# A gated layer's values projected with tokens on the partitions, and a weight split moved to GpSimd

## The chip, the cores and the metric

The kernel runs on one core of a Trainium2 chip. The metric is the device time of one execution in microseconds (us). Three runs of the kernel before took 2728.38, 2730.65 and 2730.97 us, so the median is 2730.65 us.

## The reference

Two layers over a sequence of 1024 tokens of width 1024. Layer 0 mixes with dilated attention, layer 1 with a gated recurrence (HGRN2), and each is followed by a squared-ReLU MLP; every sub-layer ends in a layer norm of a scaled residual plus its output. The change is in the gated recurrence of layer 1:

```python
def hgrn2_mixer(x, w_in, w_out, norm_g, lb):
    B, S, _ = x.shape
    H, K, V, C = HGRN_HEADS, HGRN_DK, HGRN_DV, HGRN_CHUNK    # 8, 128, 128, 64
    q_raw, f_raw, i_raw = jnp.split(x @ w_in, [H * K, 2 * H * K], axis=-1)
    z = f_raw.astype(F32)
    log_f = jnp.logaddexp(jnp.log(lb), jnp.log1p(-lb) + jax.nn.log_sigmoid(z))
    key = (1.0 - lb) * jax.nn.sigmoid(-z)
    q = jax.nn.silu(q_raw.astype(F32))
    v = i_raw.astype(F32)
    ...
    b = jnp.cumsum(log_f, axis=3)                  # within each chunk of 64 tokens
    q_dec = q * jnp.exp(b)
    k_dec = key * jnp.exp(-b)
    a = jnp.where(causal, einsum('bhcid,bhcjd->bhcij', q_dec, k_dec), 0.0)
    o_intra = einsum('bhcij,bhcje->bhcie', a, v)
    kv = einsum('bhcjd,bhcje->bhcde', key * jnp.exp(b_last - b), v)
    # states: S[c+1] = decay[c] * S[c] + kv[c]
    o_inter = einsum('bhcid,bhcde->bhcie', q_dec, states)
    o = o_intra + o_inter, then an RMS norm over each head's 128 columns, times norm_g
    return o @ w_out
```

## The kernel before

Every large product is taken in three matmuls on a high and a low part: a tensor is split by ScalarE (ACT), which rounds it to the high part, and VectorE (DVE), which subtracts that from the raw tensor to get the low part (`split`, L147 to L149). The three are high x high, low x high and high x low. TensorE (PE) works through the whole program in this way: attention, its output projection with the layer norm, the first MLP, the gated layer, its output projection with the layer norm, and the second MLP. SyncE (SP) issues nearly all transfers. A scheduler fixes the order of each engine's instructions when the program is built; the chip then runs each engine's list in order and waits on semaphores. Tiles in on-chip memory come from one pool of 49 slots of 128x1024.

In the gated layer (`hgrn`, L1734) the input x lies as features on the partitions and tokens along the row, in two halves of 512 tokens. For each of the 8 heads three 512 KB weight tiles are loaded (`w_load`, tile `wr`, split into `wh` and `wl`): forget gate z, query q and value v. `proj` (L176) makes each product in two slots of 24 matmuls of 128x512, one per half, so a head has six slots. ACT copies each out of PSUM (`ze`, `qe`, `vTh`). All three come out with features on the partitions. Behind the second z slot follows the gate chain on ACT and DVE (L1865 to L1888), behind the second q slot the query chain (L1889 to L1899, ending in `qe`).

The work per head that needs these results is made in pieces (`head_pieces`, L1743), which are run one slot each beside the next head's projections: `trans` turns `vTh` and the decayed key (tile `ze`) with 8 PE transposes each (PSUM tile `hpt`) and two ACT copies each (into `vn` and `k2n`); `amat` makes the masked scores (`as`, copied under a mask into `aT` by DVE); `kv` makes 15 outer products (`kvps`), which DVE adds up into 15 states (`stA`, `stB`, L1777 to L1781); `omats` makes the output from `aT`, `vn` and the states (`ho`), followed by the RMS norm on ACT and DVE (`sq`, `rms`, `on`); `otr` transposes that (`opt`) and ACT scales it into `oN`, which for the first five heads is stored to DRAM and loaded again later (`onr`).

The output projection (`Out`, `outproj_ln`) needs `oN` of all heads as the stationary operand, split into `hoh` and `hol`, and the output weights, split in halves of 512 columns into `woh` and `wol` from the raw tile `wor`. While the last head's pieces are still outstanding, `stage_a` multiplies by the first `NKA[1]` = 7 heads only, and `tick` (L1148) puts the outstanding pieces between its groups of three matmuls; `fin` (L1209) adds the remaining heads and makes the layer norm. `NKA` = (6, 7) holds the number for the attention and the gated layer.

## Time and profile before

| | |
|---|---|
| median of three runs | 2730.65 us |
| the profiled execution | 2730.97 us |
| its span, from its first to its last instruction | 2729.2 us |
| TensorE busy | 2699.1 us (99%) |
| VectorE, ScalarE, GpSimd busy | 2052.6 (75%), 1404.6 (51%), 189.7 us (7%) |
| granted TensorE clock, mean | 0.999 of full speed |

The 1.77 us between the execution's time and its span lie outside the instructions. In the rows below the gated layer's projections run from about 1666 to 2006 us and its output projection from there to about 2107 us, on the span's own clock. A row of a timeline has a start, a duration, the engine, the line and the tiles (output <- inputs). A duration of a matmul is longer than its step to the next one, since they overlap in the array: what a matmul costs is the difference of two starts. A wait is given in square brackets with its releaser.

### The profile page before, as it was taken

To read this page: it belongs to the slowest core of one execution; us is meant where nothing else is said; L and a number is where in the kernel's file an instruction comes from. 1 tells how busy PE (TensorE), PEld (TensorE's weight loads), DVE (VectorE), ACT (ScalarE), POOL (GpSimd) and SP (SyncE) were. 2 spreads that over 40 slices of the span, in tenths; PEclk is the share of its full clock that TensorE was granted. 3 is DMA by queue.
4 is the path that set the end of the run, shared out by engine and by line. 5 is a ranking of instruction groups with operands and counts; after the bars stand their busy time and mean duration, and the time that the engine had idled before them with its cause. 6 is when DMAs were issued, how large, how long until landed. Compare 5 with 4: busy or idle time off the path is not lost.

```text
span 2729.2 us, 41117 instructions
## 1 busy us (share of the span) xinstructions
PE 2699.1 (99%) x14600; PEld 2229.9 (82%) x14600; DVE 2052.6 (75%) x3948; ACT 1404.6 (51%) x3021; POOL 189.7 (7%) x366
## 2 busy tenths in 40 slices
PE   8999999999999999999999999999999999999998
PEld 6888888888888778888888888888888888888887
DVE  7778878778788778776687686666578786677687
ACT  5655555555555626444554344555553644454443
POOL 1021221212122100000000000000000000000000
PEclk9999999999999999999999999999999999999999
DMA  8887868777799524554685743010232464487654
GB/s 332 278 261 226 265 193 259 231 243 246 235 302 313 185 85 168 191 193 151 204 311 188 242 147 116 32 63 32 74 128 108 151 224 166 152 298 244 220 179 126
DMA packets 215790, 529.41 MB, mean 194 GB/s; under 512 B 28096, under 2 KB 41664, under 8 KB 215584
## 3 DMA queue, kind: packets, MB, share of 16 engines
q1 hardware_dynamic: 197632, 484.64, 52.5%
q0 software_dynamic: 17952, 42.14, 5.4%
q8 instruction: 115, 1.88, 0.3%
q14 instruction: 91, 0.75, 0.1%
HBM read 402.63 MB, written 98.44 MB: 184 GB/s over the span
## 4 chain that ended last, share of the span: by engine, by line
PE 91%; DVE 4%; issue 2%; DMA 1%; ACT 1%; POOL 0%; SPq 0%; DVEq 0%; POOLq 0%; ACTq 0%
PE pmm L792 8%; PE pmm L794 8%; PE pmm L793 8%; PE pup L1342 7%; PE pup L1344 7%; PE pup L1343 7%; PE pdy L1489 4%; PE pdy L1492 4%; PE pdy L1493 4%; PE pdx L1489 3%; PE pdx L1492 3%; PE pdx L1493 3%; PE pmm L182 3%; PE pmm L184 3%; PE pmm L183 3%
## 5 line engine op out<-in xcount | busy, mean ns | idle before, releaser
L792 PE MATMUL pmm<-xh,H 128*128 128x512 f32 x1008 | 401.9, 399 | 10.2 <-ACT H L496 6.5
L793 PE MATMUL pmm<-xl,H 128*128 128x512 f32 x1008 | 394.6, 391 | 4.0 <-DVE xl L149 4.0
L794 PE MATMUL pmm<-xh,H 128*128 128x512 f32 x1008 | 395.2, 392 | 1.3 <-DVE H L505 1.1
L792 PEld LDWEIGHTS pmm<-xh,H 128*128 128x128 f32 x1008 | 190.1, 189 | 59.5 <-issue 8.5
L794 PEld LDWEIGHTS pmm<-xh,H 128*128 128x128 f32 x1008 | 189.9, 188 | 43.7 <-DVE H L505 3.4
L793 PEld LDWEIGHTS pmm<-xl,H 128*128 128x128 f32 x1008 | 190.4, 189 | 42.7 <-DVE xl L149 4.6
L1489 PE MATMUL pdy<-dT,dS 128*128 128x512 f32 x512 | 199.2, 389 | 0.0
L1492 PE MATMUL pdy<-dT,dS 128*128 128x512 f32 x512 | 199.2, 389 | 0.0
L1493 PE MATMUL pdy<-dT,dS 128*128 128x512 f32 x512 | 199.2, 389 | 0.0
L182 PE MATMUL pmm<-f0nh,wh 128*128 128x512 f32 x384 | 152.3, 397 | 0.0
L148 ACT ACTIVATE dS<-dr 128x512 fp32r<-128x512 f32 x192 | 119.2, 621 | 60.0 <-PE pdy L1493 25.9
L183 PE MATMUL pmm<-f0nl,wh 128*128 128x512 f32 x384 | 149.8, 390 | 0.0
L184 PE MATMUL pmm<-f0nh,wl 128*128 128x512 f32 x384 | 149.8, 390 | 0.0
L607 ACT ACTIVATE p<-p,stats 128x256 f32<-128x256 f32 (+1 forms) x256 | 118.3, 464 | 55.0 <-DVE stats L604 54.4
L149 DVE TENSOR_TENSOR dS<-dr,dS 128x512 fp32r<-128x512 f32 x192 | 131.6, 685 | 16.9 <-ACT dS L148 16.3
L148 ACT ACTIVATE dT<-dr 128x512 fp32r<-128x512 f32 x128 | 79.3, 624 | 86.6 <-DVE dr L1462 51.7
L604 DVE CUSTOM_DVE_ANT_0 p<-s,mask 128x256 f32<-128x256 f32 (+1 forms) x256 | 82.4, 377 | 44.9 <-PE s L576 44.9
L1303 ACT ACTIVATE H<-wc 128x512 fp32r<-128x512 f32 x128 | 76.9, 625 | 72.3 <-DVE wc L1296 42.1
L1493 PEld LDWEIGHTS pdy<-dT,dS 128*128 128x128 f32 x512 | 96.1, 188 | 20.0
L1489 PEld LDWEIGHTS pdy<-dT,dS 128*128 128x128 f32 x512 | 96.1, 188 | 20.0
L1492 PEld LDWEIGHTS pdy<-dT,dS 128*128 128x128 f32 x512 | 96.1, 188 | 19.9
L867 POOL DMA_DIRECT2D rot<-e x176 | 86.3, 496 | 281.2 <-DVE e L827 50.8
(438 smaller groups left out, 6905.1 us busy)
## 6 DMA issues: line engine op xcount, KB each, us to landing
xh<-xtd SPq DMA_DIRECT2D x138, 512.0 KB, 6.3
xl<-xtd SPq DMA_DIRECT2D x138, 512.0 KB, 6.5
dr<-hd SPq DMA_DIRECT2D x192, 256.0 KB, 4.0
dr<-in_w_down_dram SPq DMA_DIRECT2D x160, 256.0 KB, 4.8
wa<-in_w_up_dram SPq DMA_DIRECT2D x48, 512.0 KB, 3.8
rot<-e POOLq DMA_DIRECT2D x176, 128.0 KB, 6.4
wb<-in_w_attn_dram SPq DMA_DIRECT2D x36, 512.0 KB, 6.3
wa<-in_w_attn_dram SPq DMA_DIRECT2D x33, 512.0 KB, 5.5
```

The lines of the kernel that those rows point to most:

```text
L148: act(hi, raw, AF.Copy)
L182: nc.tensor.matmul(o, wh[:, k], xs.h(k), start=k == 0, stop=False)
L183: nc.tensor.matmul(o, wh[:, k], xs.l(k), start=False, stop=False)
L184: nc.tensor.matmul(o, wl[:, k], xs.h(k), start=False, stop=k == NK - 1)
L792: nc.tensor.matmul(o, wh, hi[k // 2][:, c], start=begin and k == 0, stop=False, skip_group_check=True)
L793: nc.tensor.matmul(o, wh, lo[k // 2][:, c], start=False, stop=False, skip_group_check=True)
L794: nc.tensor.matmul(o, wl, hi[k // 2][:, c], start=False, stop=end and k == 3, skip_group_check=True)
L1342: nc.tensor.matmul(o, wh, xf.h(b, k), start=begin and k == 0, stop=False, skip_group_check=True)
L1343: nc.tensor.matmul(o, wh, xf.l(b, k), start=False, stop=False, skip_group_check=True)
L1489: nc.tensor.matmul(o[q], h, T_[:, L], start=begin, stop=False, skip_group_check=True)
L1492: nc.tensor.matmul(o[q], h, T_[:, R], start=False, stop=False, skip_group_check=True)
L1493: nc.tensor.matmul(o[q], l, T_[:, L], start=False, stop=end, skip_group_check=True)
```

## The change

The weight columns for the values are taken out of the per-head tiles. They are handed in as a second tensor `w_hgrn_i`, in two batches of four heads; each batch is four 512 KB tiles (`wir`, split into `wih` and `wil`) that hold two of the eight blocks of 128 input features by 512 value columns. A new function `values(batch, t)` takes 128 tokens of x as the stationary operand and 512 value columns of four heads as the moving one, so the values come out with tokens on the partitions; eight calls make a batch, each with 24 matmuls of 128x512 and one ACT copy into `vn`. The transposes of `vTh` and their copies go. The first batch runs in head 0's slots (four token blocks ahead of its z and q, four behind), the second at the head of head 4; other heads have four slots. The pieces of a head now take seven slots and run over into the head after the next; one list of six steps is left for the output projection.

`NKA[1]` becomes 5, and heads 5 and 6 are taken into `stage_a` as their output is there. The second halves of the output weights are loaded and split within the first `stage_a`, and the low half of each output weight in the gated layer is made by GpSimd (POOL) instead of DVE, 16 subtractions of 128x512 in all. In the first MLP the tile that is loaded ahead is the first of the values' tiles.

```diff
-NKA = (6, 7)
+NKA = (6, 5)
...
             nc.sync.dma_start(raw[:, c], self.w_dram[k][:, c])
-            split(raw[:, c], hi[:, c], lo[:, c])
+            act(hi[:, c], raw[:, c], AF.Copy)
+            (nc.gpsimd if self.mixer else nc.vector).tensor_sub(lo[:, c], raw[:, c], hi[:, c].bitcast(F32))
...
-        for k in range(nka):
-            pr.split_w(k, 1)
+        if not pr.mixer:
+            for k in range(nka):
+                pr.split_w(k, 1)
...
                     tick()
+                if len(tiles) > 1 and pr.mixer:
+                    pr.split_w(k, 1)
...
-            self.order = [(hd, t) for hd in range(8) for t in (1, 0, 2)]
+            self.order = [(hd, t) for hd in range(8) for t in (1, 0)]
+            self.wi = {}
...
+        def prefetch_i(self, batch, u):
+            if (batch, u) not in self.wi:
+                self.wi[batch, u] = w_load(w_hgrn_i[batch][:, u * 1024:(u + 1) * 1024], "wi")
...
                     nc.tensor.matmul(kb[c % 2][:, (t % 4) * P:(t % 4 + 1) * P], st["k2n"][r, t * P:(t + 1) * P],
-                                     st["vn"][r, t * P:(t + 1) * P], start=True, stop=True, skip_group_check=True)
+                                     val(hd, t)[r], start=True, stop=True, skip_group_check=True)
...
-                if hd < SPILL[1] and j == 1:
-                    nc.sync.dma_start(ond[1, hd], oNt)
+                if j == 1:
+                    if hd < SPILL[1]:
+                        nc.sync.dma_start(ond[1, hd], oNt)
+                    oN.append(ond[1, hd] if hd < SPILL[1] else oNt)
...
             return [
-                [lambda: trans(vT, "vn"), lambda: amat(0), lambda: amat(1), lambda: trans(kd2, "k2n")],
+                [],
+                [lambda: trans(kd2, "k2n")],
+                [lambda: amat(0), lambda: amat(1)],
                 [lambda: kv(0), lambda: kv(1)],
-                [],
                 [omats],
                 [],
                 [lambda: otr(0), lambda: otr(1)],
-            ]
+            ][hd == 7:]
...
+        def values(batch, t):
+            if (batch, t // 2) not in vals:
+                vals[batch, t // 2] = U("vn")
+            o = bank("mm", "pmm")
+            x_, c = xs[t // 4], slice((t % 4) * P, (t % 4) * P + P)
+            for k in range(NK):
+                wh, wl = (w[:, (k % 2) * 512:(k % 2) * 512 + 512] for w in gw.wi[batch, k // 2])
+                nc.tensor.matmul(o, x_.h(k, c), wh, start=k == 0, stop=False)
+                nc.tensor.matmul(o, x_.h(k, c), wl, start=False, stop=False)
+                nc.tensor.matmul(o, x_.l(k, c), wh, start=False, stop=k == NK - 1)
+            act(vals[batch, t // 2][:, (t % 2) * 512:(t % 2) * 512 + 512], o, AF.Copy)
...
-        prefetch(0)
-        n = 0
+        for u in range(4):
+            gw.prefetch_i(0, u)
...
-            slots = [(t, h) for t in (1, 0, 2) for h in range(2)]
+            slots = [(t, h) for t in (1, 0) for h in range(2)]
             if hd == 0:
-                slots = [(1, 1), (0, 1), (2, 1), (1, 0), (0, 0), (2, 0)]
...
+                slots = [(2, 4), (2, 5), (2, 6), (2, 7), (1, 1), (0, 1), (1, 0), (0, 0), (2, 0), (2, 1), (2, 2), (2, 3)]
+            elif hd == 4:
+                slots = [(2, t) for t in range(8)] + slots
...
+                    if hd == 3:
+                        gw.prefetch_i(1, 2 * (1 - t) + h)
...
-    xs, late = ffn(0, xf, late, x1d, ln_ffn_g[0], ln_ffn_b[0], False, lambda: gw.prefetch(0),
+    xs, late = ffn(0, xf, late, x1d, ln_ffn_g[0], ln_ffn_b[0], False, lambda: gw.prefetch_i(0, 0),
...
-        "w_hgrn": cols(i["hgrn_w_in"][0]),
+        "w_hgrn": cols(i["hgrn_w_in"][0][:, :2 * D]),
+        "w_hgrn_i": i["hgrn_w_in"][0][:, 2 * D:].reshape(NK, P, 2, 512).transpose(2, 1, 0, 3).reshape(2, P, NK * 512),
```

On SP, at the start of the gated layer, the kernel before has this, where `wr` is a weight tile and `x3d` the first MLP's stored output:

```order
610 L1525 DMA x3d<-z 128x1024
611 L153 DMA wr<-in_w_hgrn_dram 128x1024
612 L1740 DMA smask<-in_smask_dram 128x1024
613 L1525 DMA x3d<-z 128x1024
614 L153 DMA wr<-in_w_hgrn_dram 128x1024 x2
615 L1525 DMA x3d<-z 128x1024
616 L153 DMA wr<-in_w_hgrn_dram 128x1024 x5
```

The changed kernel has, at the same place:

```order
610 L1530 DMA x3d<-z 128x1024
611 L154 DMA wir<-in_w_hgrn_i_dram 128x1024
612 L1750 DMA smask<-in_smask_dram 128x1024
613 L1530 DMA x3d<-z 128x1024
614 L154 DMA wir<-in_w_hgrn_i_dram 128x1024 x2
615 L1530 DMA x3d<-z 128x1024
616 L154 DMA wir<-in_w_hgrn_i_dram 128x1024
617 L154 DMA wr<-in_w_hgrn_dram 128x1024 x7
```

The four value tiles stand where the first four weight tiles stood, the fourth behind a store of `x3d`, and the weight tiles follow behind them.

On PE, where the last head's projections end, the kernel before goes over from `wh` and `wl` to the output weights `woh` and `wol` like this; `opt` and `as` belong to heads 6 and 7, `hpt` to head 7:

```order
7608 L184 MATMUL pmm<-f0nh,wl 128x512
7609 L1820 MATMUL opt<-ident,on 128x128 x8
7610 L1760 MATMUL as<-qe,ls 128x128 x8
7611 L194 MATMUL pmm<-woh,hoh 128x512
7612 L195 MATMUL pmm<-wol,hoh 128x512
...
7617 L196 MATMUL pmm<-woh,hol 128x512 x2
7618 L1752 MATMUL hpt<-ident,vTh 128x128 x8
7619 L196 MATMUL pmm<-woh,hol 128x512
```

In the changed kernel head 6's outer products `kvps` and its output `ho` stand at this place, the latter in pieces between three to six matmuls of the output projection:

```order
7591 L185 MATMUL pmm<-f0nh,wl 128x512
7592 L1782 MATMUL kvps<-vn,k2n 128x128 x15
7593 L195 MATMUL pmm<-woh,hoh 128x512
7594 L196 MATMUL pmm<-wol,hoh 128x512
7595 L197 MATMUL pmm<-woh,hol 128x512
7596 L1800 MATMUL ho<-vn,aT 128x128 x4
7597 L1804 MATMUL ho<-stA,qe 64x128 x5
7598 L195 MATMUL pmm<-woh,hoh 128x512
7599 L196 MATMUL pmm<-wol,hoh 128x512
7600 L1804 MATMUL ho<-stA,qe 64x128
```

Head 6's outer products and output, which ran beside head 7's projections, now run behind them, with 3 matmuls of the output projection between the two.

On DVE, the states of head 6 (`stA`, `stB`) stand ahead of head 7's gate chain (lines from L1871 on) in the kernel before:

```order
2741 L1778 COPY stA<-kvps 128x128
2742 L1780 SCALAR_TENSOR_TENSOR stA<-stA,dec,kvps 128x128 x6
2743 L1780 SCALAR_TENSOR_TENSOR stB<-stA,dec,kvps 128x128
2744 L1780 SCALAR_TENSOR_TENSOR stB<-stB,dec,kvps 128x128 x7
2745 L1871 SCALAR_TENSOR_TENSOR ls<-ze,a_18701 128x1024
2746 L1872 SCALAR_TENSOR_TENSOR ze<-ze,a_18701 128x1024
2747 L1876 TENSOR_SCALAR ls<-ls,hc_C,hc_A 128x1024
```

In the changed kernel they stand behind it, and two splits of the head outputs (`hol`) stand between:

```order
2743 L1917 TENSOR_TENSOR ls<-ls,a_18609 128x1024
2744 L1918 SCALAR_TENSOR_TENSOR a_18609<-smask,ls 128x1024
2745 L150 TENSOR_TENSOR hol<-onr,hoh 128x512
2746 L1921 TENSOR_TENSOR ze<-ze,a_18609 128x1024
2747 L150 TENSOR_TENSOR hol<-onr,hoh 128x512
2748 L1924 TENSOR_TENSOR ze<-a_18609,ze 128x1024
2749 L1788 COPY stA<-kvps 128x128
2750 L1790 SCALAR_TENSOR_TENSOR stA<-stA,dec,kvps 128x128 x6
2751 L1790 SCALAR_TENSOR_TENSOR stB<-stA,dec,kvps 128x128
```

The states of head 6 have moved from ahead of head 7's gate chain to behind it.

## Rows read from the trace of the kernel before

**Rows 1.** The page: busy us, share of the span and instructions per engine.

```profile
PE 2699.1 (99%) x14600; PEld 2229.9 (82%) x14600; DVE 2052.6 (75%) x3948; ACT 1404.6 (51%) x3021; POOL 189.7 (7%) x366
```

**Rows 2.** TensorE's waits, 1660 to 2110: releaser, us in total, times, longest.

```profile
PE as L1760 <- DVE qe L1898: 0.9, 1, 0.9
PE pmm L196 <- DVE hol L149: 0.4, 1, 0.4
```

**Rows 3.** Busy us (instructions) of the engines by stretch, granted clock, DMA share, GB/s.

```profile
core 0: us, PE busy (x) PEld busy (x) DVE busy (x) ACT busy (x) POOL busy (x), PEclk, DMA share, GB/s
1500.00:1600.00 100.00, 100.00 (x443) 82.83 (x442) 78.52 (x137) 41.66 (x82) 0.00 (x0) 1.00 0.67 222
1793.00:1836.00 43.00, 43.00 (x261) 36.51 (x260) 26.01 (x44) 23.59 (x34) 0.00 (x0) 1.00 0.13 47
...
2060.00:2110.00 50.00, 50.00 (x236) 40.90 (x235) 45.99 (x94) 15.55 (x41) 0.00 (x0) 1.00 0.38 140
```

**Rows 4.** PE timeline, heads 0 and 1: start, us, engine, line, operation, tiles, count.

```profile
1705.95 1.03 PE L1752 MATMUL hpt<-ident,vTh 128*128 128x128 f32 x8
1706.74 0.48 PE L182 MATMUL pmm<-f0nh,wh 128*128 128x512 f32 x1
1707.07 0.40 PE L183 MATMUL pmm<-f0nl,wh 128*128 128x512 f32 x1
...
1750.38 1.03 PE L1752 MATMUL hpt<-ident,vTh 128*128 128x128 f32 x8
1751.25 0.94 PE L1760 MATMUL as<-qe,ls 128*128 128x128 f32 x7
```

**Rows 5.** PE timeline at 1710, head 0: the wait for its query.

```profile
1710.28 0.39 PE L182 MATMUL pmm<-f0nh,wh 128*128 128x512 f32 x1
1711.55 1.16 PE L1760 MATMUL as<-qe,ls 128*128 128x128 f32 x8 [0.88 <-DVE qe L1898]
```

**Rows 6.** PE timeline at 2007, the first output projection tiles.

```profile
2007.28 0.39 PE L195 MATMUL pmm<-wol,hoh 128*128 128x512 f32 x1
2008.03 0.73 PE L196 MATMUL pmm<-woh,hol 128*128 128x512 f32 x2 [0.36 <-DVE hol L149]
```

**Rows 7.** PE timeline in head 6: eight score products, fifteen state products, next projection.

```profile
1988.68 1.95 PE L1790 MATMUL ho<-vn,aT 128*128 128x128 f32 x16
1990.56 0.98 PE L1794 MATMUL ho<-stA,qe 128*64 128x128 f32 x13
...
1992.45 0.50 PE L182 MATMUL pmm<-f0nh,wh 128*128 128x512 f32 x1
```

**Rows 8.** DVE by line, 1793 to 1837: count, busy us, mean ns, idle.

```profile
L1878 DVE TENSOR_TENSOR_SCAN a<-smask,ls 128x1024 f32<-128x1024 f32 x1 | 2.3, 2291 | 0.0
```

**Rows 9.** ACT by line in the same stretch.

```profile
L1753 ACT ACTIVATE vn<-hpt 128x512 f32<-128x512 f32 x2 | 1.1, 597 | 0.0
```

**Rows 10.** DVE timeline in head 6: first states, then the gate chain.

```profile
1976.88 0.29 DVE L1778 COPY stA<-kvps 128x128 f32<-128x128 f32 x1 [6.71 <-PE kvps L1772]
1977.29 2.26 DVE L1780 SCALAR_TENSOR_TENSOR stA<-stA,dec,kvps 128x128 f32<-128x128 f32 x6
...
1982.60 1.22 DVE L1871 SCALAR_TENSOR_TENSOR ls<-ze,a 128x1024 f32<-128x1024 f32 x1
```

**Rows 11.** POOL by line, whole span, and DVE's instructions on tile wol.

```profile
L1737 POOL MEMSET aT<- 128x1024 f32 x1 | 1.0, 954 | 658.5 <-DVE dT L149 658.5
masks.py:199 POOL TENSOR_SCALAR_AFFINE_SELECT ident<-ident 128x128 f32<-128x128 f32 x1 | 0.3, 285 | 0.0
...
L149 DVE TENSOR_TENSOR wol<-wor,woh x32: 667/687/693, 898.4 to 2035.9; 128x512 fp32r<-128x512 f32 x32
```

**Rows 12.** 512 KB weight tiles: landing, and SP's issues at the stage's start.

```profile
DMA to landing us min/median/max: 3.3/5.3/6.3
...
1661.67 1.21 SPq L153 DMA_DIRECT2D wr<-in_w_hgrn_dram  x2
...
1673.34 2.90 SPq L153 DMA_DIRECT2D wr<-in_w_hgrn_dram  x4
```

More of the change, by code (lines that the diff above doesn't have):

```diff
@@ L81, in trunk_kernel @@
     w_hgrn: bass.AP,
+    w_hgrn_i: bass.AP,
     w_hgrn_out: bass.AP,
@@ L1789, in omats @@
                     cs = slice(t % 4 * P, (t % 4 + 1) * P)
-                    nc.tensor.matmul(os[t // 4][:, cs], aTs[t // 4][:, cs], st["vn"][:, t * P:(t + 1) * P],
+                    nc.tensor.matmul(os[t // 4][:, cs], aTs[t // 4][:, cs], val(hd, t),
                                      start=t % 4 == 0, stop=False, skip_group_check=True)
@@ L1834, in hgrn @@
         oN = []
         pend = []
-        prefetch(0)
-        n = 0
+        for u in range(4):
+            gw.prefetch_i(0, u)
         for hd in range(8):
             e = {}
-            slots = [(t, h) for t in (1, 0, 2) for h in range(2)]
+            slots = [(t, h) for t in (1, 0) for h in range(2)]
             if hd == 0:
-                slots = [(1, 1), (0, 1), (2, 1), (1, 0), (0, 0), (2, 0)]
-                for i in range(3):
-                    prefetch(i)
+                slots = [(2, 4), (2, 5), (2, 6), (2, 7), (1, 1), (0, 1), (1, 0), (0, 0), (2, 0), (2, 1), (2, 2), (2, 3)]
+            elif hd == 4:
+                slots = [(2, t) for t in range(8)] + slots
@@ L1845, in hgrn @@
             seen = set()
             cur = {}
-            for t, h in slots:
-                bi = hd * 3 + (1, 0, 2).index(t)
-                prefetch(bi)
-                prefetch(bi + 1)
-                if t not in e:
-                    e[t] = U(("qe", "ze", "vTh")[t])
-                if bi == len(order) - 1 and h == 1 and hd:
-                    pre(oN)
-                o = proj(loaded[bi], xs[h])
-                act(e[t][:, h * 512:(h + 1) * 512], o, AF.Copy)
+            for n, (t, h) in enumerate(slots):
+                if t == 2:
+                    values(hd // 4, h)
+                    if n == 1:
+                        prefetch(hd * 2)
+                    if n == 2:
+                        prefetch(hd * 2 + 1)
+                else:
+                    bi = hd * 2 + 1 - t
+                    prefetch(bi)
+                    if bi % 8 != 7:
+                        prefetch(bi + 1)
+                    if t not in e:
+                        e[t] = U(("qe", "ze")[t])
+                    if hd == 7 and n == 2:
+                        pre(oN)
+                    o = proj(loaded[bi], xs[h])
+                    act(e[t][:, h * 512:(h + 1) * 512], o, AF.Copy)
+                    if hd == 3:
+                        gw.prefetch_i(1, 2 * (1 - t) + h)
@@ L1899, in hgrn @@
                     cur["qd"] = q
-            for i in range(3):
-                del loaded[hd * 3 + i]
+            for i in range(2):
+                del loaded[hd * 2 + i]
+            if hd % 4 == 0:
+                for u in range(4):
+                    del gw.wi[hd // 4, u]
             oNt = U("oN")
-            oN.append(ond[1, hd] if hd < SPILL[1] else oNt)
-            new = head_pieces(hd, cur["kd"], cur["kd2"], cur["qd"], e[2], cur["dec"], oNt)
-            pend = [(pend[i] if i < len(pend) else []) + new[i] for i in range(len(new))]
+            new = head_pieces(hd, cur["kd"], cur["kd2"], cur["qd"], cur["dec"], oNt)
+            pend = [(pend[i] if i < len(pend) else []) + (new[i] if i < len(new) else [])
+                    for i in range(max(len(pend), len(new)))]
         return oN, pend
```

5 lines of the change are left out of this document (4 added, 1 removed).

## The prediction

> **What bounds the kernel now.** I read the page first, then TensorE's waits, then the timeline where the change acts. The reader is to see that TensorE is busy for 2699.1 of 2729.2 us [rows 1], that in steady work its matmuls of 128x512 follow each other at 100 / 443 = 0.226 us at a granted clock of 1.00 [rows 3], and that in the whole stretch from 1660 to 2110 us, which holds the gated layer and its output projection, it waits twice, for 0.9 and 0.4 us [rows 2]. So within the stage only three things change the time: instructions of TensorE that go, these two waits, and new waits. VectorE is busy 26.0 of 43 us beside one head's projections, and ScalarE 23.6 [rows 3]: their work there is covered, and what is taken off them is worth nothing by itself. Behind the projections that is otherwise: from 2060 to 2110 VectorE is busy 46.0 of 50 us [rows 3].
>
> **Transposes.** The 8 transposes of `vTh` take 1751.25 - 1750.38 = 0.87 us where other small products follow, and 1706.74 - 1705.95 = 0.79 us alone, behind which the next matmul takes 0.33 instead of 0.23 us, so 0.89 [rows 4]. There is one such block per head: 8 x 0.87 = 7.0 us gone. The 384 matmuls for the values stay 384 of the same shape: 16 value blocks of 24 against 8 heads x 2 x 24. The 16 ACT copies of 597 ns [rows 9] go too, 9.6 us of an engine that is not awaited: nothing. The weight splits keep their number. In the steady heads a slot holds a small block as before, four per head, so the borders stay.
>
> **The two old waits.** Head 0's scores wait for `qe`: 1711.55 - 1710.28 = 1.27 us to the next start, less 0.23 for the matmul and 0.1 for the border, 0.95 us [rows 5]. After, four value blocks (4 x 5.4 us of matmuls) stand between head 0's query and its scores, so that wait goes: -0.95. Behind it the next head's query is not late: a head still has 96 matmuls, 21.7 us, and small products; the chain of 1024-wide steps and the 2.29 us scan [rows 8] that ran beside 43 us of work must fit into about 31.5, of which VectorE's work fills an estimated 27 (the 26.0 us of rows 3 with the third weight's share added). I take no wait there and 3 us as the far end. The wait at 2007.28 for the low half of a head's output, 2008.03 - 2007.28 - 0.23 = 0.5 us [rows 6], stood behind a subtraction of a weight on VectorE; with that on GpSimd it goes: -0.5.
>
> **Start of the stage.** The first value block needs all four value tiles, where the first z slot needed one. Tile 4 is issued where 1673.34 stands now, behind a store of `x3d` [rows 12]. It lands 3.3 to 6.3 us later, so at 1676.6 to 1679.6, is then split (about 2 us), and is needed when 6 of 8 feature blocks of three token blocks, which the scheduler has interleaved, are through: about 54 matmuls and the layer-norm transposes, some 14 us behind 1666, near 1680. I take +0.5 us between 0 and +5.
>
> **Small blocks that split up.** At the end of the projections `ho`, `as` and `opt` stand in pieces between single matmuls. I count 12 blocks against 8. A border costs 0.1 on leaving [rows 4] and at most as much on entering: +0.8, between 0.4 and 1.2.
>
> **End of the projections.** Here lies the uncertain term. With T the end of the last projection, head 6's `kvps`, `ho` and head 7's pieces now all stand behind it, where only head 7's stood. On TensorE 15 outer products (taken like the 15 state products, 1992.45 - 1990.56 = 1.9 us [rows 7]), 3 matmuls (0.7) and 4 score products (half of 1990.56 - 1988.68, 0.9 [rows 7]) put the first five state products at T + 3.5, done at T + 4.2. On VectorE the states now stand behind head 7's gate chain. That chain starts when z is out of PSUM, 14 us before T (two slots of 5.4, the blocks 0.9 and 2.8), runs through six ACT steps of about 1.1 us with the two `k2n` copies and two weight copies between, so that the scan starts near T - 2.4 and ends near T - 0.1; then two `hol` at 0.69 and two 1024-wide steps at 1.22 [rows 10, 11] end near T + 3.7. The copy (0.29) and four more states at 2.26 / 6 = 0.38 [rows 10] come at T + 5.6. What waits is 5.6 - 4.2 = 1.4 us, and up to 2.5 if an ACT step comes later; I take 2.0. Queued behind these state products are head 7's transposes and the whole output projection. Next, head 7's query: its chain ends near T + 15.3 on VectorE, behind head 6's norm, and its scores are due near T + 14.7: 0.65 (0 to 1.5). Then one weight's high half, late on ACT behind the query chain, 0.3, and head 7's `kvps`, which need a PSUM bank that ACT has to empty, one copy of 0.6 us: 0.65.
>
> **The lower halves on GpSimd.** The trace of before has no subtraction on GpSimd. The nearest rows are half of a 128x1024 memset, 0.48 us, and four times the 128x128 select, 1.14 us; VectorE takes 0.687 us for the same subtraction [rows 11]. A second input could double the select's: 2.3 us. Between 0.48 and 2.3 I take 1.2, near the select, which like it reads its data. Of the 16, those for the third head's first half and the fifth head's second half are needed within about 1 us of ACT's high half: 1.7 us of waiting at 1.2 (0 at 0.48, 4.6 at 2.3). The others have several matmul groups in front. By the Trainium skill, GPSIMD Engine Reference, section 3.1 (Elementwise — side-by-side cycle accounting), an add of two fp32 tensors took 1.96 times VectorE's time, since the two inputs share a read port; by that a subtraction here would be an estimated 1.35 us, and the two waits 2.0 instead of 1.7. No run here shows it yet.
>
> **Sum.** -7.0 - 0.95 - 0.5 + 0.5 + 0.8 + (2.0 + 0.65 + 0.3 + 0.65 + 1.7 = 5.3) = -1.85 us against the profiled execution's 2730.97 (span 2729.2 and 1.77 outside): 2729.1. The median of before is 2730.65, 0.3 lower than that execution, so I say 2729.0 us. About 0.2%, 5.5 us, is what a measurement of this kernel can tell from no change; this lies within.
>
> **Rivals.** *The cover holds.* The scheduler has ordered the pieces so that each state, query and low half is there in time, and the end of the projections costs 1 us instead of 5.3. For it: TensorE waited only 0.4 us there before [rows 2], and VectorE is rid of 16 x 0.687 = 11 us. Against it: the states stand behind the gate chain. The time would be 2729.0 - 4.3 = 2724.7, and 2722.5 with no wait and no new border: faster. *GpSimd and VectorE hold each other up* (slower). Each subtraction on GpSimd lengthens whatever two-input work VectorE has beside it. Of the 16, about 10 fall into the 25 us behind T, where VectorE is already what TensorE waits for; if each holds VectorE for its own 1.2 us, 12 us come on top of 5.3, some of it taken up by VectorE's lost 11 us of subtractions only later: 2729.0 + 8 to 12 = 2737 to 2741. From 7 us of such holding on, the change is slower. For it: VectorE's list there is one chain; against it: no row shows the two engines at work together. The Trainium skill, GPSIMD Engine Reference, section 1 (Specifications), says that GpSimd shares its SBUF interfaces with VectorE and that they contend with instructions of two SBUF inputs, which speaks for this rival; no row here bears it out or against it. *The start is late.* Tile 4 lands at the slow end and each tile's split queues behind the layer norm on VectorE: +5 instead of +0.5, 2733.5, still no change. *The values gain nothing*, because with x stationary the matmuls have another pitch: 384 x 0.01 us would be 4; both forms load 128x128 weights and move 512 columns, so I give it next to nothing.
>
> **How the numbers follow.** Forecast with its own spread (2725.2 to 2736.1): 0.52. The cover holds, or nearly: 0.25. GpSimd holds VectorE up: 0.15. Late start: 0.08, which counts as no change. So faster 0.25, same 0.60, slower 0.15. The range is 2722.5 (no new wait at all) to 2737.5 (just into the slower rival, and what all the upper ends of the known terms but the start's come to: -8.45 + 0.5 + 1.2 + 2.5 + 1.5 + 0.6 + 1.3 + 4.6 = 3.75 above the forecast's start from 2730.97, so 2734.7, with half of the late start).
>
> **What would show it.** In the trace after, the `hpt` blocks from `vTh` are gone and with them the wait for `qe` near 1711. TensorE's waits between the last projection and the layer norm name VectorE's `stA`, `qe` or the `wol` on GpSimd, in sum about 5 us; under 2 the first rival is right. The mean of the 16 `wol` on GpSimd is near 1.2 us, and VectorE's rows of 1024 beside them keep 1.22 us; if they grow, the second rival is right. A wait on `wih` or `wil` within the first 20 us of the stage shows the third. I am wrong in the main point if the states are in time, or if the steady heads wait at all.

## The result, and the profile after

The changed kernel takes 2740.59 us (median of 7 runs, 2738.18 to 2741.56) against 2730.65 us of the kernel before (7 runs, 2727.06 to 2735.45): a ratio of 1.0034, with a 95% interval of 1.0025 to 1.0044. The forecast was 2729.0 us within 2722.5 to 2737.5, no change. It is slower by 9.9 us.

The time ahead of the gated layer varies by some 10 us between executions in which that part is the same (the layer's first projection starts between 1661.4 and 1670.9 us in the profiles of this case), while all that follows the layer's output projection takes 622.2 to 622.9 us in each. So kernels are compared below also by their *stage*: from the start of the first projection matmul of the gated layer to that of the last `wol` matmul of its output projection. The start of the last projection matmul divides it into the *projections* and the *end*. A stage is read from one profiled execution per kernel. Each ratio below is against the kernel before as measured again beside that run (medians 2730.03 to 2731.56 us); the change of the median and that of the stage differ by up to 2.2 us.

| kernel | projections | end | stage, us | median time, us |
|---|---|---|---|---|
| before | 336.6 | 103.7 | 440.3 | 2730.65 |
| after | 331.5 | 119.7 | 451.2 | 2740.59 |

The page's busy row of after shows what of the work changed:

```profile
PE 2699.4 (99%) x14536; PEld 2223.9 (81%) x14536; DVE 2054.4 (75%) x3932; ACT 1400.0 (51%) x3005; POOL 213.4 (8%) x382
```

TensorE has 64 instructions less than in [rows 1], the transposes; ScalarE has 16 less, VectorE 16 less, GpSimd 16 more. TensorE's waits in 1660 to 2120, where [rows 2] had two:

```profile
PE ho L1800 <- DVE stB L1790: 5.6, 5, 1.5
PE kvps L1782 <- ACT oN L1831: 2.2, 1, 2.2
PE pmm L196 <- POOL wol L1093: 2.0, 2, 1.1
PE pmm L197 <- DVE hol L150: 2.0, 2, 1.1
PE pmm L1859 <- ACT wih L149: 0.9, 1, 0.9
PE as L1770 <- DVE qe L1938: 0.6, 1, 0.6
```

The first row is five waits in the steady heads (the six whose output lies within the projections), where the prediction had none. TensorE's timeline in one of them (start, duration, engine, line, tiles):

```profile
1757.97 2.05 PE L1782 MATMUL kvps<-vn,k2n 64*128 64x128 f32 x30
...
1765.52 1.05 PE L1800 MATMUL ho<-vn,aT 128*128 128x128 f32 x8
1767.69 1.16 PE L1800 MATMUL ho<-vn,aT 128*128 128x128 f32 x8 [1.12 <-DVE stB L1790]
1768.78 0.98 PE L1804 MATMUL ho<-stA,qe 128*64 128x128 f32 x13
```

The output starts 7.55 us behind the outer products, where it was 13.0 us in the kernel before: there the outer products are the row below, and the output starts at 1988.68 [rows 7].

```profile
1975.69 2.05 PE L1772 MATMUL kvps<-vn,k2n 64*128 64x128 f32 x30
```

In the changed kernel the output's second half waits for VectorE, whose timeline beside it is:

```profile
1757.74 2.29 DVE L1918 TENSOR_TENSOR_SCAN a<-smask,ls 128x1024 f32<-128x1024 f32 x1
1760.06 1.23 DVE L1921 TENSOR_TENSOR ze<-ze,a 128x1024 f32<-128x1024 f32 x1
1761.21 0.28 DVE L1788 COPY stA<-kvps 128x128 f32<-128x128 f32 x1
1761.61 1.12 DVE L1790 SCALAR_TENSOR_TENSOR stA<-stA,dec,kvps 128x128 f32<-128x128 f32 x3
1762.64 1.22 DVE L1924 TENSOR_TENSOR ze<-a,ze 128x1024 f32<-128x1024 f32 x1
1763.77 1.11 DVE L1790 SCALAR_TENSOR_TENSOR stA<-stA,dec,kvps 128x128 f32<-128x128 f32 x3
1764.92 0.35 DVE L1790 SCALAR_TENSOR_TENSOR stB<-stA,dec,kvps 128x128 f32<-128x128 f32 x1
1765.37 2.65 DVE L1790 SCALAR_TENSOR_TENSOR stB<-stB,dec,kvps 128x128 f32<-128x128 f32 x7
```

The reader is to see that the gate chain (the scan and the two steps on `ze`) stands ahead of the states and within them, that the states end at 1768.02, that the second block of score products starts at 1767.69, and that this block uses no state. Of the seven states in the last row the sixth ends at 1767.64 and the seventh starts behind it, so what the block waits for is set free by the last state but one; in all five heads the block starts 0.05 or 0.06 us behind that state. The whole output takes 5.15, 4.96, 5.68, 5.15 and 4.95 us in these heads instead of 3.77 in the kernel before: 7.0 us in all. The sixth steady head is head 3, whose pieces stand beside value blocks, with no gate chain on VectorE. Its output too follows 7.55 us behind its outer products (at 1864.40), but VectorE stands idle when the outer products come, so the states begin at once, there is no wait, and the output takes 3.77 us:

```profile
1858.03 0.29 DVE L1788 COPY stA<-kvps 128x128 f32<-128x128 f32 x1 [4.71 <-PE kvps L1782]
```

Behind the projections the other waits of the list come to 6.8 us with those too short for it. The longest is head 6's outer products, which need a PSUM bank that ScalarE empties with `oN`:

```profile
2000.21 2.18 PE L1782 MATMUL kvps<-vn,k2n 64*128 64x128 f32 x24 [2.17 <-ACT oN L1831]
```

```profile
1999.35 0.23 ACT L1927 ACTIVATE dec<-a 128x16 f32<-128x16 f32 x1 [2.74 <-DVE a L1918]
1999.49 1.25 ACT L1831 ACTIVATE oN<-opt,hg 128x512 f32<-128x512 f32 x2
```

ScalarE's list runs in order, and `oN` stands behind `dec`, which waits for the scan in head 7's gate chain on VectorE. That scan runs from 1996.05 to 1999.32 (the first row of the next block), past the start of the last projection matmul at 1997.02. In the kernel before it ended at 1993.33, 9.9 us ahead of that matmul (2003.24):

```profile
1991.04 2.29 DVE L1878 TENSOR_TENSOR_SCAN a<-smask,ls 128x1024 f32<-128x1024 f32 x1
```

The 16 subtractions on GpSimd have a duration of min/median/max 1267/1303/2267 ns, with a mean of 1.50 us. VectorE, and below it GpSimd:

```profile
1996.05 3.27 DVE L1918 TENSOR_TENSOR_SCAN a<-smask,ls 128x1024 f32<-128x1024 f32 x1
...
2003.79 2.27 DVE L1790 SCALAR_TENSOR_TENSOR stA<-stA,dec,kvps 128x128 f32<-128x128 f32 x6
...
2011.64 2.18 DVE L1936 TENSOR_TENSOR a<-a,a 128x1024 f32<-128x1024 f32 x1
2013.75 1.77 DVE L150 TENSOR_TENSOR hol<-onr,hoh 128x512 fp32r<-128x512 f32 x1
...
2019.11 1.24 DVE L1817 TENSOR_TENSOR rms<-rms 128x4 f32<-128x4 f32 x1
...
2021.63 1.21 DVE L1819 TENSOR_SCALAR rms<-rms 128x4 f32<-128x4 f32 x1
```

```profile
1995.17 2.00 POOL L1093 TENSOR_TENSOR wol<-wor,woh 128x512 fp32r<-128x512 f32 x1 [0.24 <-ACT woh L1092]
2003.30 1.31 POOL L1093 TENSOR_TENSOR wol<-wor,woh 128x512 fp32r<-128x512 f32 x1 [6.13 <-ACT woh L1092]
2010.95 4.02 POOL L1093 TENSOR_TENSOR wol<-wor,woh 128x512 fp32r<-128x512 f32 x2 [6.34 <-ACT woh L1092]
2018.54 5.50 POOL L1093 TENSOR_TENSOR wol<-wor,woh 128x512 fp32r<-128x512 f32 x4 [3.57 <-ACT woh L1092]
```

VectorE rows that start beside a subtraction are up to 1.1 us longer than elsewhere: the scan 3.27 against 2.29 us [rows 8], an addition of 1024 columns 2.18 against 1.22 [rows 10], a `hol` 1.77 against 0.69, and an instruction of four columns 1.24 against 0.16 (in the first experiment). The four-column instruction ends at 2020.35, the subtraction beside it at 2020.33, and the next three end 0.01 to 0.03 us behind a subtraction too. Not all rows grow: the states from 2003.79, which read `kvps` in PSUM, begin beside the subtraction of 2003.30, which lasts past the third of them, and take 2.27 us for six, against 2.26 [rows 10].

### The profile page after: what moved, and what is told of

Its sections match the earlier page's. It is cut to its first block, busy times and chain, and to the rows that moved or that the text cites. A ratio compares the mean times of both kernels' runs of the same rounds, so it can differ in the third digit from the quotient of the medians.

```text
span 2739.2 us, 41013 instructions
## 1 busy us (share of the span) xinstructions
PE 2699.4 (99%) x14536; PEld 2223.9 (81%) x14536; DVE 2054.4 (75%) x3932; ACT 1400.0 (51%) x3005; POOL 213.4 (8%) x382
## 4 chain that ended last, share of the span: by engine, by line
PE 56%; DVE 4%; issue 3%; ACT 2%; DMA 1%; POOL 0%; SPq 0%; DVEq 0%; POOLq 0%; ACTq 0%
PE pup L1347 7%; PE pup L1349 7%; PE pup L1348 7%; PE pdy L1494 4%; PE pdy L1497 4%; PE pdy L1498 4%; PE pdx L1494 3%; PE pdx L1497 3%; PE pdx L1498 3%; PE pmm L197 2%; PE pmm L196 2%; PE pmm L195 2%; PE pmm L1859 1%; PE pmm L1860 1%; PE pmm L183 1%
## 5 line engine op out<-in xcount | busy, mean ns | idle before, releaser
L183 PE MATMUL pmm<-f0nh,wh 128*128 128x512 f32 x256 | 101.6, 397 | 0.0
L185 PE MATMUL pmm<-f0nh,wl 128*128 128x512 f32 x256 | 99.8, 390 | 0.0
L184 PE MATMUL pmm<-f0nl,wh 128*128 128x512 f32 x256 | 99.8, 390 | 0.0
```

The lines of the kernel that those rows point to most:

```text
L183: nc.tensor.matmul(o, wh[:, k], xs.h(k), start=k == 0, stop=False)
```

## The experiments

Each edit is against the changed kernel where nothing else is said; "low halves on VectorE" and "swap" name the first two from there on.

**The low halves on VectorE again.**

```diff
-            (nc.gpsimd if self.mixer else nc.vector).tensor_sub(lo[:, c], raw[:, c], hi[:, c].bitcast(F32))
+            nc.vector.tensor_sub(lo[:, c], raw[:, c], hi[:, c].bitcast(F32))
```

> The changed kernel with the 16 low halves of the output weights made by VectorE again. In the trace after, VectorE's instructions beside a subtraction on GpSimd are about 1 us longer than elsewhere (the scan 3.27 instead of 2.29 us, a 1024-wide addition 2.18 instead of 1.22, an instruction of 4 columns 1.24 instead of 0.16). Theory 1 (GpSimd holds VectorE up, about 1 us per subtraction, some 8 of them where TensorE waits for VectorE): these rows return to 2.29, 1.22 and 0.16 us, TensorE's waits behind the last projection fall by 2 to 5 us, time 2736 to 2738.5 us. Theory 2 (the long rows are chance or harmless, the order of the pieces is all that costs): VectorE now has 16 x 0.69 = 11 us more to do there, time 2740.5 to 2744 us.

Measured: 2739.7 us (8 runs), ratio 1.0029 (1.0019 to 1.004); projections 331.7, end 117.0, stage 448.7 us. VectorE's rows return to their lengths:

```profile
1991.91 2.29 DVE L1918 TENSOR_TENSOR_SCAN a<-smask,ls 128x1024 f32<-128x1024 f32 x1
...
2009.64 1.22 DVE L1936 TENSOR_TENSOR a<-a,a 128x1024 f32<-128x1024 f32 x1
...
2011.38 0.16 DVE L1817 TENSOR_TENSOR rms<-rms 128x4 f32<-128x4 f32 x1
```

So GpSimd does hold VectorE up; taking it away shortens the stage by 2.5 us. TensorE's waits behind the last projection fall from 6.8 to 3.1 us, as theory 1 has it, and that on `oN` is gone. But the small blocks split up more there: in its timeline TensorE changes over between them and the large matmuls 46 times instead of 36. The median fell by 0.9 us, and 2739.7 lies 1.2 us above theory 1's window: by the whole time alone the theories are not told apart, by the rows and the stage they are.

**The outer products' PSUM banks swapped.**

```diff
-                kb = [bank("s" if j else "pt", "kvps") for _ in range(2)]
+                kb = [bank("pt" if j else "s", "kvps") for _ in range(2)]
```

> The changed kernel, with the two halves of the 15 outer products in each other's PSUM banks: the first eight in the two banks that were the second half's, and the reverse. In five of the steady heads the output's second block of score products waits 0.9 to 1.5 us for VectorE's last state. Theory 1 (it waits for the PSUM bank of the second half's outer products, which VectorE frees with its last state; the states' own values would be there in time or nearly): the wait goes to 0 to 0.4 us per head, the blocks of 5.0 to 5.7 us return to 3.8 to 4.2, time 2733 to 2736 us. Theory 2 (the states themselves are late, the bank is only the first to show it): the same time is then lost ahead of the products with the states stB, time 2739 to 2741.5 us.

Measured: 2732.74 us (11 runs), ratio 1.0007 (0.9998 to 1.0016); projections 325.7, end 117.2, stage 442.9 us. The head shown above now reads:

```profile
1764.08 1.95 PE L1800 MATMUL ho<-vn,aT 128*128 128x128 f32 x16
1765.95 0.98 PE L1804 MATMUL ho<-stA,qe 128*64 128x128 f32 x13
```

The 16 products of the scores run through, although VectorE's states end no earlier, relative to the outer products, than in the changed kernel (10.07 us behind their start, 10.05 there). What was waited for is the PSUM bank: the output's second half takes a bank of the pair `s`, in which the second half's outer products lay until VectorE had read them. These alternate between two banks, so one bank is read out with the last state but one, which is where the block started. Theory 1 holds; the time is 0.3 us under its window. The states themselves are only just in time: here the last ends at 1766.59 and the first product that uses `stB` starts at 1766.66. One steady head still takes 5.05 us: its states begin late, and the bank now holds the first half's outer products (0.5 us of wait on `stA`). The swap moves 8.4 us of the stage, 5.8 in the projections, all of it in the outputs, and the rest in the end, where TensorE's waits are 4.0 us instead of 6.8.

**The low halves on GpSimd in the kernel before, alone.**

```diff
-            split(raw[:, c], hi[:, c], lo[:, c])
+            act(hi[:, c], raw[:, c], AF.Copy)
+            (nc.gpsimd if self.mixer else nc.vector).tensor_sub(lo[:, c], raw[:, c], hi[:, c].bitcast(F32))
```

> The kernel before with one part of the change alone: the gated layer's 16 low halves on GpSimd. Theory 1 (each subtraction of some 1.3 to 2 us on GpSimd holds VectorE up by about 1 us): VectorE's instructions beside them are longer by about 1 us each, some 10 us in sum; as VectorE is also rid of 11 us and TensorE waited 0.4 us there before, TensorE's new waits are 0 to 4 us, time 2730 to 2735 us. Theory 2 (no holding up): VectorE's rows keep their lengths, TensorE's waits stay under 1.5 us, time 2729.5 to 2732 us.

Measured: 2734.23 us (11 runs), ratio 1.001 (1.0001 to 1.0019); projections 336.7, end 106.6, stage 443.3 us, 3.0 more than before, as theory 1 has it. TensorE's wait names GpSimd, and VectorE's subtractions beside it take 4.78 / 3 = 1.6 us each instead of 0.69:

```profile
PE pmm L195 <- POOL wol L1092: 2.0, 2, 1.5
```

```profile
2008.69 4.78 DVE L149 TENSOR_TENSOR hol<-onr,hoh 128x512 fp32r<-128x512 f32 x3 [0.33 <-ACT hoh L148]
```

**One empty slot between outer products and output.**

```diff
                 [lambda: kv(0), lambda: kv(1)],
+                [],
                 [omats],
```

> The changed kernel with one empty slot put back between a head's outer products and its output, as the kernel before had it; a head's pieces then take eight slots. Theory 1 (a slot of 5.4 us is too short for the states, which in the kernel before had two): the waits of the five steady heads, 5.6 us, and what goes with them, 7 us in all, are gone; the end of the projections gets one piece more to do; time 2731 to 2736 us. Theory 2 (VectorE has too much work per head for the shorter head, wherever the output stands): the wait moves to the transposes or scores of the next head, time 2739 to 2742 us.

Measured: 2738.97 us (6 runs), ratio 1.0029 (1.0018 to 1.0041); projections 329.9, end 118.9, stage 448.7 us. The old wait went and another came, as theory 2 has it, but neither at the place nor for the reason that it names: the transposes of the output now share a slot with the next outer products, and both use the bank pair `pt`, which ScalarE empties:

```profile
PE kvps L1782 <- ACT oN L1831: 5.1, 4, 2.5
```

**Swap and low halves on VectorE together.** Both edits above.

> The changed kernel with both the swapped PSUM banks of the outer products and the low halves on VectorE. The swap alone gave 2732.7 us, with 1.1 + 0.45 us of waits on GpSimd and 1.7 + 1.1 us on VectorE and ScalarE behind the projections left. Theory 1 (GpSimd costs here what it costs alone in the kernel before, 3 us): 2729 to 2731 us, from the stage's first matmul to the output projection's last about 439 to 441 us instead of 442.7. Theory 2 (VectorE's own work is what the end of the projections waits for, so 11 us more of it take the gain back): 2732 to 2734.5 us.

Measured: 2732.26 us (11 runs), ratio 1.0006 (0.9997 to 1.0015); projections 325.9, end 116.9, stage 442.8 us. The time and the stage of theory 2: with the swap, taking GpSimd's work away gains nothing (442.9 with it). Its reason isn't shown. TensorE's waits in the end fall from 4.0 to 2.3 us, now mostly on `hoh` and `hol`, the splits of the heads' outputs, while the small blocks split up more: 50 changeovers instead of 40, and 10.3 instead of 9.5 us in `ho`. Writing the second halves' splits ahead of the output projection again, as before, on top of these two edits gave 2732.0 us (11 runs) and 442.6, within the 1.5 us of that run's first theory: they don't matter.

**Head 0's z and q first** (on top of swap and low halves on VectorE). Their two weight tiles are loaded ahead of the value tiles, too, which the lines here leave out.

```diff
-                slots = [(2, 4), (2, 5), (2, 6), (2, 7), (1, 1), (0, 1), (1, 0), (0, 0), (2, 0), (2, 1), (2, 2), (2, 3)]
+                slots = [(1, 1), (0, 1), (2, 4), (2, 5), (2, 6), (2, 7), (1, 0), (0, 0), (2, 0), (2, 1), (2, 2), (2, 3)]
```

> As the run before, and head 0 begins with its two z and q blocks, so that one weight tile is enough for the first matmuls and the four value tiles are needed only 11 us later. Theory 1 (the 0.9 to 1.1 us wait for the third and fourth value tile at the stage's start is the price of the order there): this wait is gone, nothing replaces it, 1 us less than the run before, 2728 to 2730 us. Theory 2 (the weights come at the same rate, so the wait moves to the first value block or to the following heads): the same time as the run before within 0.5 us.

Measured: 2733.82 us (11 runs), ratio 1.001 (1.0002 to 1.0019); stage 442.8 us, as without this edit, though the median is 1.6 us longer. Theory 2: the wait of 0.9 us on `wih` became one of 0.8 on `wil`, at the first value block.

**Head 6's output a step later** (on top of that).

```diff
-        return oN, pend
+        return oN, [[]] + pend
```

> As the second run of these, with one empty step put ahead of the pieces that are left for the output projection, so that head 6's output stands 18 matmuls (4 us) behind its outer products instead of 3. Theory 1 (the end of the projections costs what it costs because head 6's output follows its outer products at once, while VectorE is still in head 7's gate chain): TensorE's waits behind the projections fall by 2 to 4 us against the second run, 2725 to 2727.5 us, and this is the first version clear of the kernel before. Theory 2 (VectorE and ScalarE have too much to do there in any order): the wait moves to head 7's scores or output, within 1 us of the second run.

Measured: 2729.63 us (11 runs), ratio 0.9994 (0.9985 to 1.0003); end 114.5 instead of 116.9, stage 440.3 us. The direction of theory 1 and part of its size. It is not the named waits that fall (3.5 us after 2.3), but the time in the pieces of `ho`, from 10.3 to 7.5 us, and the number of changeovers, from 50 to 32. Of the 10.8 us that stay against 103.7, some 5 are head 6's outer products and output, which moved here.

**Another order of the pieces** (on top of swap and low halves on VectorE, without the last two edits).

```diff
-                [],
-                [lambda: trans(kd2, "k2n")],
-                [lambda: amat(0), lambda: amat(1)],
-                [lambda: kv(0), lambda: kv(1)],
-                [omats],
-                [],
+                [lambda: trans(kd2, "k2n")],
+                [lambda: kv(0), lambda: kv(1)],
+                [lambda: amat(0), lambda: amat(1)],
+                [omats],
+                [],
+                [],
                 [lambda: otr(0), lambda: otr(1)],
-            ][hd == 7:]
+            ]
```

> The values as in the change, low halves on VectorE, banks of the outer products swapped, and the pieces of a head in another order: transposes, outer products, scores, output, two empty slots, transposes of the output. So a slot with the scores stands between outer products and output, and head 6 is through but for its last transposes when the projections end. Theory 1 (of the 10 us lost, some 7 came from the output one slot behind the outer products, the rest from head 6's outer products and output moved behind the projections, where VectorE and ScalarE do not keep up): from the stage's first matmul to the output projection's last 434 to 437 us instead of 440.3 before and 442.8 with the swap, time 2724 to 2728 us, faster than the kernel before. Theory 2 (the saved transposes are lost again because VectorE has too much work per shorter head): the wait turns up at the scores or at the transposes of the decayed key, 439 to 443 us, 2729 to 2733 us.

Measured: 2732.57 us (11 runs), ratio 1.0009 (1.0 to 1.0018); projections 328.8, end 113.7, stage 442.5 us. Head 6's outer products now lie within the projections again and its output directly behind them, yet the end is only 3 us shorter: a miss for theory 1. The time and the stage are theory 2's, and 1.9 us of waits stand at the transposes of the decayed key, which it names. The longest wait is another:

```profile
PE pmm L195 <- ACT hoh L149: 3.2, 1, 3.2
```

Behind it TensorE is slower for a while. The columns are those of [rows 3], with the granted clock third from the end:

```profile
2006.40:2012.00 5.60, 5.36 (x11) 3.57 (x12) 5.60 (x10) 3.76 (x7) 0.00 (x0) 0.50 0.42 128
```

The clock is 0.50 of full speed, the 1.2 GHz level, and matmuls of 512 columns follow each other at 0.43 instead of 0.23 us, so these 5.4 busy us cost an estimated 2.5 us more than at 1.00. The same order without the swap took 2732.82 us (11 runs) and 442.4, as that run's second theory has it: with the outer products that early their bank is free in time. This order with the swap and the low halves on GpSimd:

> As the first of these runs, with the 16 low halves on GpSimd as in the change. Theory 1 (each subtraction on GpSimd holds VectorE up by about 1 us and takes twice as long itself, and that costs where TensorE waits for one of both): 1.5 to 4 us slower than the first run. Theory 2 (with head 6 out of the way both engines have time to spare): within 1 us of the first run.

Measured: 2740.17 us (5 runs), ratio 1.0041 (1.0027 to 1.0055); end 119.5, stage 448.3 us. GpSimd costs 5.8 us here, more than either theory has, 2.5 and 3.0 in the first and third experiment, and nothing beside the swap (442.9 against 442.8): it depends on what TensorE waits for. Part of the 5.8 us is the clock: it is 0.50 for two stretches here, with 8.9 us of TensorE's work instead of 5.4, an estimated 1.6 us.

**The kernel before, with head 7's values first.** Only the order of head 7's six slots is altered, so that its query comes last, as in the change.

```diff
+            if hd == 7:
+                slots = [(t, h) for t in (2, 1, 0) for h in range(2)]
...
-                if bi == len(order) - 1 and h == 1 and hd:
+                if t == 0 and h == 1 and hd == 7:
```

> The kernel before, where head 7 alone projects its values first, then z and q, so that its last projection is the query, as in the change; nothing else is altered. Theory 1 (the two value slots, 11 us of matmuls, covered head 7's chains on ScalarE and VectorE and the output projection's splits; without them TensorE waits): the stretch from the last projection to the output projection's last matmul grows from 103.7 to 109 to 114 us, time 2735 to 2741 us. Theory 2 (the end of the projections is slow in the change for the pieces' order alone): within 1.5 us of the kernel before.

Measured: 2740.53 us (5 runs), ratio 1.0034 (1.0022 to 1.0047): as slow as the whole change. Projections 337.9, end 112.2 instead of 103.7, stage 450.1 us, as theory 1 has it. TensorE stands still behind the projections, and ScalarE's list shows why:

```profile
2007.66 1.04 PE L1820 MATMUL opt<-ident,on 128*128 128x128 f32 x8
2014.03 0.80 PE L194 MATMUL pmm<-woh,hoh 128*128 128x512 f32 x1 [5.33 <-ACT hoh L148]
```

```profile
2008.15 0.23 ACT L1889 ACTIVATE dec<-a 128x16 f32<-128x16 f32 x1 [3.10 <-DVE a L1880]
...
2012.31 1.15 ACT L1887 ACTIVATE ze<-ze,hc_C 128x1024 f32<-128x1024 f32 x1 [0.25 <-DVE ze L1886]
2013.36 1.13 ACT L148 ACTIVATE hoh<-onr 128x512 fp32r<-128x512 f32 x2
```

The splits that the output projection needs first stand behind head 7's gate chain, which itself waits for VectorE's scan. Before, two value slots, 11 us of matmuls, lay over this. ScalarE stands still for 3.10 us at `dec` here and for 2.74 us in the changed kernel: the same wait for the same scan, with `hoh` behind it here and `oN` there. Of the 8.5 us that the end grows by, 5.0 are wait (5.33 for 0.36), and behind it the clock is low until 2017.95, which costs an estimated 1.8 us of its 3.9:

```profile
2014.00:2017.90 3.90, 3.87 (x13) 3.30 (x14) 1.29 (x2) 3.84 (x6) 0.00 (x0) 0.50 0.27 68
```

In the changed kernel it stays at 1.00 behind its wait of 2.17 us:

```profile
2000.30:2008.00 7.70, 7.70 (x56) 5.62 (x57) 6.25 (x14) 5.06 (x7) 1.31 (x1) 1.00 0.45 139
```

**The splits taken out from behind the chain.** On the other order of the pieces, with the splits of four heads and weights in head 6's third slot, and of three in its first:

```diff
-NPRE = 2
+NPRE = 3
...
-                    if hd == 7 and n == 2:
+                    if hd == 6 and n == 0:
                         pre(oN)
```

> As the run with the outer products first (442.5 us from the stage's first matmul to the output projection's last, 113.7 of it behind the last projection), but the splits of four instead of two heads' outputs and output weights are written in head 6 instead of in head 7's third slot. Theory 1 (these splits stand behind head 7's chains): the 3.2 us wait for hoh goes, the stretch behind the last projection falls to 107 to 110 us, some of it is given back in heads 6 and 7, time 2727 to 2730 us. Theory 2 (ScalarE and VectorE are full there, wherever the splits stand): 112 to 115 us, time 2731 to 2734 us.

> As the run before with three heads' splits, written in head 6's first slot. Theory 1: the stretch behind the last projection 108 to 111 us, less given back in the heads than with four, time 2726 to 2729 us, clear of the kernel before. Theory 2: as above, 2731 to 2734 us.

Measured: with four 2730.37 us (11 runs), ratio 0.9996 (0.9988 to 1.0005), projections 334.8, end 106.2, stage 441.1 us; with three (the edit shown) 2728.86 us (11 runs), ratio 0.9987 (0.9978 to 0.9996), projections 331.4, end 107.3, stage 438.8 us. The end falls by 6 to 7 us, as theory 1 has it, and the heads give back 3 to 6. The clock stays at 1.00 in both, so an estimated 2.5 of these 6 to 7 us are the low clock of the other order that no longer comes. With three, the waits left are short, this the largest in total:

```profile
PE hpt L1762 <- ACT ze L1925: 3.0, 4, 1.4
```

This version beats the kernel before by 0.13%, just clear of its interval (1.5 us by the stage), and the changed kernel by some 12 us.

## Why the prediction was wrong

The sum that the runs give for the stage, against the one that was forecast: transposes -7.0 (forecast -7.0); head 0's query -0.95 (-0.95); start +0.9 (+0.5); steady heads +7.0 (0); the end, beside the pieces moved there: 16.0 - (1.98 + 3.76 for head 6's `kvps` and `ho`, less 0.79 for one block of transposes) = +11.0 (5.3 and 0.8 for borders, less 0.5 for the old wait). Together 10.95, and the stage grew by 10.9 us. By its own sign the prediction is wrong in the main point: the steady heads wait.

- **Transposes, query, start.** Right in place, and in size within the bounds. The wait at the start is on `wih` for 0.9 us, where 0.5 was taken between 0 and 5; the rival of a late start did not come.
- **Steady heads: the step that failed.** "I take no wait there" compared busy sums, 27 of 31.5 us, and asked only whether the next query would be late. The busy sum was about right (25.0 and 27.7 us in the two heads from 1765.52 on). But the change also cuts the distance from outer products to output from 13.0 to 7.55 us and leaves the gate chain ahead of the states, and the second half of the output takes a PSUM bank that those outer products hold until VectorE's last state but one. That is a deadline of one slot for a buffer, which no sum of busy time shows. The swap shows that it is the bank: with the states no earlier, 5.8 of the 7.0 us go. Head 3 shows that the gate chain belongs to it: the same distance without that chain, and no wait.
- **The end: the term of 5.3 us was mis-sized, at half its value, and its cause was named in part.** Of the 11.0 us, 6.4 are waits (6.8 for 0.4) and 4.6 lie in small blocks: 36 changeovers instead of 26, and longer `kvps` and `ho`. Of the priced waits, GpSimd's is 2.0 (forecast 1.7) and the query's 0.60 (0.65), the latter by luck, since the scores come at T + 20 and not at T + 14.7. The states, priced at 2.0, are no row in the list of waits: head 6's first ten state matmuls run in step with VectorE, each pair just behind a state, from 2004.12 to 2005.71, in 1.59 us where ten of thirty take 0.63 [rows 7], so the states cost some 1.0, within the 4.6. What was not seen is what else stands behind head 7's gate chain. Its scan was put at T - 2.4 to T - 0.1 and ran from T - 1.2 to T + 2.1, 1.0 us of that held by GpSimd, and ScalarE's `oN` behind it kept head 6's outer products waiting for 2.2 us; a bank that ScalarE has to empty was priced at 0.65, for head 7's. Two waits on `hol`, 2.0 us, were not forecast either. Behind this is that the last two slots before the end had been values, work that needs no chain behind it, and are now z and q. Taking that cover away in the kernel before alone adds 8.5 us to its end, by the same wait of ScalarE; how much of the 11.0 us it makes in the changed kernel, where other work fills part of the time and the clock doesn't fall, is not shown by itself.
- **GpSimd.** The duration was nearly right: 1.30 us median and 1.50 mean against 1.2 taken. By the Trainium skill, GPSIMD Engine Reference, section 3.1 (Elementwise — side-by-side cycle accounting), it was an estimated 1.35, and the median agrees. The slower rival's mechanism is there too: VectorE's rows grow by up to 1.1 us beside a subtraction. The Trainium skill, GPSIMD Engine Reference, section 1 (Specifications), names contention with VectorE instructions in a 2-port perf mode or with two SBUF inputs. The rows that grew with two operands in SBUF agree. The `TENSOR_SCALAR` of four columns, which has one tensor input, was held for 1.21 instead of 0.17 us as well, and no run here shows in which mode it ran. But the rival's price of 8 to 12 us was too high: 2.5 us in the changed kernel, where VectorE's own 0.69 us per subtraction goes in exchange and six subtractions, not ten, begin in the 25 us behind T. That its time, 2737 to 2741 us, holds the measured 2740.6 is a coincidence, since GpSimd accounts for about a quarter of the loss.

What stays open: the parts are not additive. Swap and VectorE together gave 442.8 us where their gains apart add up to 451.2 - 8.4 - 2.5 = 440.3. The named waits do fall; the small blocks split up more instead, and which order the scheduler gives them for an edit was not tested by itself. The clock also differs: it is 0.50 for a while in the end with the swap alone (3.3 us of TensorE's work), with the empty slot (6.1), with values first in the kernel before (3.9), and in the three runs of the other order that keep the splits behind the chain (5.4, 2.9 and 8.9). In the stage of all other runs, the kernel before and the changed one among them, it is 1.00. So differences of 1 to 4 us between the experiments' ends can be the clock's; the 10.9 us of the change are not.

## What to carry to other kernels

When a change shortens the distance between two steps, look for every buffer that the later one reuses and who empties it, not only for the data. Before moving work away from the end of a stage, ask what it covered there: the last work ahead of a dependent stage should be the one that nothing waits behind. An engine with spare time is not free when its instructions lengthen those of the one it is to relieve. And before the length of a stretch is put down to an edit, look at the granted clock in it: a wait can cost more than it lasts.

## What the runs showed of the hardware

A subtraction of 128x512 on GpSimd lasted 1.27 to 2.27 us. VectorE's instructions on SBUF that began beside one lasted up to 1.1 us longer whatever their size: 3.27 instead of 2.29 us for the scan, 1.24 instead of 0.16 us for four columns, and those of four columns ended when the subtraction did, within 0.03 us. States that read PSUM beside a subtraction kept their length (2.27 us for six). With no work on GpSimd there, the same rows of the same program had their usual lengths.

TensorE's granted clock fell to 0.50 (1.2 GHz) within a wait of 5.33 us in the kernel before with values first and within one of 3.22 us in the other order of the pieces, and was 1.00 again from 2017.95 and 2012.03 on. It stayed at 1.00 behind a wait of 2.17 us in the changed kernel, but was 0.50 from 1994.0 to 1997.3, behind a wait of 1.70 us that ended at 1992.98, in the run with the swap.
